# A hybrid decoder step on one core: prompt attention's steps taken two by two, w_in's blocks in another order, the cached sums moved into a triangular product, and the first sequence's rows fetched during prompt attention

## The chip, the cores and the metric

The kernel runs on one core of one Trainium2 chip. The metric is the device time of one execution in microseconds (us), median of the runs shown. The profile comes from one further execution of the same program.

## What is computed

One inference step of a one-layer decoder for a prompt of 512 tokens and for 8 sample sequences of 8 new tokens each, whose 2048 cached tokens lie in pages of 128. Both groups share the weights (D_MODEL 1024, 8 heads of 64, two key/value groups for each attention). The reference, cut to what matters here:

```python
mod = silu(c) @ w_ada + b_ada                       # six parts: shift, scale, gate, twice
h = rms_norm(x) * (1 + sc1) + sh1
z = h @ w_in                                        # fox q,k,v,f; nsa q, kv (6 parts), gates; two merge gates
logf = log_sigmoid(ff + b_fox_f)
fox:  softmax(q k / 8 + cumsum(logf)_q - cumsum(logf)_k) v         # causal
nsa:  gate0 * compressed + gate1 * selected + gate2 * window       # each a softmax with alibi bias
mix = g_fox * (o_fox @ w_br_fox) + g_nsa * (o_nsa @ w_br_nsa)
x = x + gt1 * (mix @ w_out)
y = x + gt2 * (relu(h2 @ w_up) ** 2 @ w_down)
```

The prompt has only 8 selection blocks for 16 places, so its selected attention is a causal one over all tokens. For the samples the compressed scores rank the cached blocks, 16 are selected, and fox needs, for each cached token, the sum of the log forget values of all later cached tokens (a suffix sum over 2048 tokens for each head). New key and value rows are outputs too.

## The kernel before, in words

Work goes through stages. Most products are made in pairs of high and low parts (`split`, line 130).

**First stage** (`first_stage`). 32 steps u = 0..31 (keys and values in turn): page rows (tile `cpg`) are put in order (`ro`), turned (`ct`), split (`xh`, `xl`) and multiplied (`hid`) to compress the cached keys and values. A table `todo` hangs other work on the steps, behind the step's own: the norm of x, and the first 8 of w_ada's 24 blocks, 1 MB each (`wada`, two buffers). `ada_first_load` issues a block's load on SP's queue, `ada_first` multiplies it (`ada`), `ada_end` turns and adds its parts (`adat`), and `modulate` then applies two blocks to the normed x. The modulated x (`hf`, 2.3 MB) is stored for a later stage (`hfd`).

**Projection** (`run`, `project`). Eight blocks of w_in's columns in the order of `WIN` (`z` matmuls). Each block's weights are asked for one block ahead (`win_load`, tile `winr`). Between blocks lie norms of heads (`head_norm`: squares on ScalarE, the rest on VectorE), stores of new rows (SP), the prompt's compressed keys (`cmp_prompt_a` to `_e`), one more w_ada block for each step (`ada_later`), and the copying of cached fox rows, a piece for each step, into an order fit for loading (`stage`, DRAM tensors `foxD`, `lfD`).

**Prompt attention** (`prompt_attention`). Twelve steps of one branch and one pair of heads each, in the order slc 0, win 0, slc 1, win 1, ..., win 3, then fox 0 to 3. A step makes the scores of both groups (`scores`: matmuls into PSUM, VectorE adds the bias row and takes the row minimum, ScalarE the exponential); in the next step its weights are turned (`turn_over`: TensorE into PSUM, ScalarE or VectorE copies `PT` out) and multiplied with the values (`weigh`, tile `oT`). A slc step has the compressed heads besides (`cmp_heads` on VectorE, from an accumulator bank `cs`; of those there are two, tag `acc`, and `weigh` uses one or two). `kstack` and `qstack` make stacked high and low keys and queries. Into this stage are put: for the prompt, fk's norm and the log-sigmoid (step 0), `decay` and `forget_rows` (fox's bias rows, over DRAM); for the samples, `sample_kv`, `forget_load` and `forget_sums` (suffix sums of the cached log forget values in `Dt`, by four doubling passes over 1024 columns on VectorE and one product over partitions), `sample_cmp`, `sample_rank`, `sample_select`. `ada_later` goes on until block 23; its room (`adw`, tag `r2`) is free then.

**Sample attention** (`sample_tables`, `sample_attention`). Tables first (one-hot `E`, `bhot`, masks `nbA`, `nbW`, the bias `ramp`). Then for each sequence two halves of 8 pages: `sample_load` (fox rows `fr` of 1 MB by one DMA, nsa rows `sr` by eight DMAs of 128 KB, all on SP), `sample_scores` one sequence ahead, and `sample_values`. A score block gets its decay by four matmuls of `E` with the turned `Dt` (`DT`). `hf` is read back (tile `hf1b`) ahead of the first rows. Then come the merge (`mix_part`), w_out and the MLP.

What sets the order: the program is written in the order above, and the scheduler of the tile framework orders each engine's instructions by a timeline that it simulates. `issue_after` and `behind` bind an instruction behind another on the same engine. `dma` keeps SP's transfers in the order of the program, and an instruction that waits holds all that are behind it on its engine or queue.

Of the kernel before, what the change touches and what calls it, by code (L numbers as in the profile page):

```python
# [14 lines left out]
P = 128  # L15
# [29 lines left out]
class Step:  # L45
# [268 lines left out]
    def ada_later(self):  # L314

        a = self.adw
        if self.ada_next:
            self.ada_next()
        ch = self.adn
        self.ada_next = None  # L320
# [4 lines left out]
        w = a[:, 2048 * e:2048 * e + 2048].rearrange("p (k c) -> p k c", k=NK)  # L325
        self.ada_load(ch, w)

        def later():
            part = a[:, 4096 + 256 * e:4352 + 256 * e]
            self.ada_sum(ch, w, part)  # L330
            self.ada_end(ch, part, a[:, 4608 + 18 * e:4626 + 18 * e].rearrange("p (j r) -> p j r", j=2))
# [159 lines left out]
    def first_stage(self, pl, pe, hf):  # L491
# [116 lines left out]
    def forget_sums(self, pa):  # L608
# [4 lines left out]
        fl = lambda t, a, e: t[:, :, a:e, :].rearrange("p b c h -> p b (c h)")  # L613
# [4 lines left out]
        cur, nxt = sc  # L618
        tot = self.carve([P, NB, 8])
        self.cp(tot, cur[:, :, 0, :])  # L620
        xb = self.accb("xsuf")
        self.mm(xb[:, 0:64], triS, tot.rearrange("p b h -> p (b h)"), True, True)
        self.cp(tot, xb[:, 0:64].rearrange("p (b h) -> p b h", h=8))
        self.tt(nxt[:, :, 0:15, :], cur[:, :, 1:16, :], tot[:, :, None, :].to_broadcast([P, NB, 15, 8]), OP.add)
        self.cp(nxt[:, :, 15, :], tot)
        self.cp(self.Dt, nxt)
# [118 lines left out]
    WIN = ((1288, 264), (1552, 264), (1816, 264), (0, 256), (256, 256), (776, 256), (1032, 256), (512, 264))  # L745
# [52 lines left out]
    def log_sigmoid(self, pz):  # L798
# [5 lines left out]
        e, u, l1, d = [pz.tile([P, 40], F32, name=f"ls{i}") for i in range(4)]  # L804
# [120 lines left out]
    def prompt_attention(self, pk, pn, pp):  # L925
# [16 lines left out]
        kst = {"slc": self.kslc, "win": self.kstack(pp, "win", C_WK)}  # L942
        qs = {("nsa", 0): self.qnsa}
        fox = {}
        prev = pcT = None
        for br, r in [(br, r) for r in range(4) for br in ("slc", "win")] + [("fox", r) for r in range(4)]:
# [4 lines left out]
            elif br == "fox":  # L951
                rows = fox[r]
# [22 lines left out]
            if (br, r) == ("win", 0):  # L975
                qs["nsa", 1] = self.qstack(pp, "nsa", C_NQ, 1, 1)
# [907 lines left out]
```

## Time and profile before

| | us |
|---|---|
| runs before | 1404.58, 1409.5, 1407.9; median 1407.9 |
| profiled execution | 1405.54 |
| its span | 1403.8 |
| first stage | 0 to about 200 |
| projection | about 200 to 334 |
| prompt attention | about 335 to 530 |
| sample attention | about 530 to 755 |
| merge, w_out, MLP | about 755 to 1404 |

How to read it: a row of the timeline has its start, its length, engine, line, operation, output tile, input tiles, shapes and count; in brackets at its end stands how long the engine had stood idle, and behind which engine's instruction or transfer. A row of the windows has the busy time of each engine in a stretch with the number of instructions, the granted clock of TensorE (1.00 is full), the share of the DMA engines and GB/s. PE is TensorE, PEld its weight load, DVE VectorE, ACT ScalarE, POOL GpSimd, SPq the issues of SyncE's queue. L76 is the helper for matmuls and L82 that for turns, so tiles tell more than lines.

### The profile page before, as it was taken

The numbers are of one execution on the slowest core, as the hardware profiler recorded it, in microseconds if no ns is written. First come the engines' busy times: TensorE is split into PE (matmuls) and PEld (weight loads), VectorE is DVE, ScalarE is ACT, GpSimd is POOL, SyncE is SP. The second block draws the span as 40 slices with busy tenths as digits, with TensorE's granted clock in tenths as the row PEclk, the third lists the DMA queues.
The fourth block names the chain that finished last, engine by engine and source line by source line (L and its number), as shares of the span: only waits on it lengthen the run. The fifth ranks groups of instructions, "written<-read, shape, count | busy, mean of one in ns | idle before, by whom it ended". The sixth has DMA issues, their size and how long they took to land.

```text
span 1403.8 us, 23571 instructions
## 1 busy us (share of the span) xinstructions
PE 1296.2 (92%) x8787; PEld 1060.3 (76%) x8787; DVE 729.5 (52%) x1910; ACT 504.5 (36%) x1097; POOL 89.9 (6%) x89
## 2 busy tenths in 40 slices
PE   1897999997898977999999999998899999999998
PEld 0776789896555543555558999998888998998997
DVE  3576675458756684344336433377523443443464
ACT  2344353245655642223226222232432321321320
POOL 0000000002211210000000000000100100100110
PEclk9999999998998988999999999999999999999999
DMA  9576256752235537565553533140422321331401
GB/s 206 164 220 191 78 177 224 249 194 93 82 106 148 154 134 249 201 210 192 198 165 102 133 83 91 53 121 1 150 63 74 116 77 49 120 89 33 120 31 68
DMA packets 167832, 182.78 MB, mean 130 GB/s; under 512 B 15813, under 2 KB 153326, under 8 KB 163366
## 3 DMA queue, kind: packets, MB, share of 16 engines
q1 hardware_dynamic: 162406, 178.14, 41.3%
q10 hardware_dynamic: 5312, 3.15, 1.0%
q8 instruction: 69, 1.13, 0.3%
q14 instruction: 45, 0.37, 0.1%
HBM read 169.99 MB, written 28.54 MB: 141 GB/s over the span
## 4 chain that ended last, share of the span: by engine, by line
PE 77%; SPq 6%; DMA 6%; DVE 6%; ACT 2%; issue 2%; POOL 0%; DVEq 0%; ACTq 0%
PE dn L76 14%; PE up L76 14%; PE mg L76 7%; PE z L76 7%; SPq L154 6%; PE ss L76 5%; PE hid L76 4%; PE br L76 4%; PE so L76 4%; PE wo L76 3%; PE ada L76 2%; PE ct L82 1%; DMA cpg<-in_cache_nsa_kv 1%; DMA sr<-in_cache_nsa_kv 1%; PE sp L82 1%
## 5 line engine op out<-in xcount | busy, mean ns | idle before, releaser
L76 PE MATMUL dn<-wdh,u 128*128 128x512 f32 x576 | 181.9, 390 | 0.0
L76 PEld LDWEIGHTS dn<-wdh,u 128*128 128x128 f32 x576 | 107.6, 188 | 21.9
L76 PE MATMUL dn<-wdl,u 128*128 128x512 f32 x320 | 123.6, 389 | 0.0
L76 PE MATMUL z<-winh,h 128*128 128x264 f32 (+1 forms) x576 | 113.1, 289 | 1.9 <-DVE h L708 1.7
L76 PE MATMUL up<-h,wuh 128*128 128x256 f32 x512 | 96.7, 282 | 4.3 <-ACT h L111 4.3
L76 PEld LDWEIGHTS z<-winh,h 128*128 128x128 f32 x576 | 93.2, 192 | 4.6 <-DVE h L708 2.9
L76 PE MATMUL z<-winl,h 128*128 128x264 f32 (+1 forms) x320 | 88.9, 286 | 0.0
L111 ACT ACTIVATE wdh<-wdr 128x1024 fp32r<-128x1024 f32 x32 | 33.1, 1054 | 148.6 <-PE dn L76 127.7
L76 PE MATMUL up<-h3H,wuh 128*128 128x320 f32 x256 | 80.6, 315 | 6.2 <-ACT wuh L111 6.2
L130 DVE TENSOR_TENSOR wul<-wur,wuh 128x1024 fp32r<-128x1024 f32 x32 | 48.9, 1534 | 70.9 <-ACT wuh L111 70.9
L99 DVE TENSOR_TENSOR acc<-acc,dn 128x512 f32<-128x512 f32 x60 | 40.3, 686 | 86.5 <-PE dn L76 86.5
L76 PEld LDWEIGHTS up<-h,wuh 128*128 128x128 f32 x512 | 81.4, 191 | 4.5 <-ACT h L111 4.5
L76 PE MATMUL up<-h3H,wul 128*128 128x320 f32 x256 | 80.1, 313 | 0.3 <-DVE wul L130 0.3
L76 PE MATMUL up<-h3L,wuh 128*128 128x320 f32 x256 | 79.9, 312 | 0.0
L76 PE MATMUL mg<-hH,wmh 128*128 128x288 f32 x256 | 75.4, 295 | 0.8 <-ACT hH L111 0.8
L76 PE MATMUL mg<-hL,wmh 128*128 128x288 f32 x256 | 74.6, 296 | 0.6 <-DVE hL L130 0.6
L76 PE MATMUL mg<-hH,wml 128*128 128x288 f32 x256 | 75.2, 294 | 0.0
L76 PE MATMUL up<-h,wul 128*128 128x256 f32 x256 | 72.1, 282 | 0.0
L1674 POOL TENSOR_TENSOR u<-u 128x576 f32<-128x576 f32 x32 | 43.5, 1361 | 439.5 <-ACT u L111 434.3
L82 PE MATMUL ct<-identF,ro 128*128 128x128 f32 x256 | 38.3, 297 | 35.4 <-DVE ro L114 29.8
L111 ACT ACTIVATE xh<-ct 128x256 fp32r<-128x256 f32 x128 | 47.7, 385 | 63.8 <-PE ct L82 41.7
L76 PEld LDWEIGHTS dn<-wdl,u 128*128 128x128 f32 x320 | 60.1, 188 | 12.6
(663 smaller groups left out, 3126.0 us busy)
## 6 DMA issues: line engine op xcount, KB each, us to landing
adw<-in_w_ada SPq DMA_DIRECT2D x16, 1024.0 KB
foxD<-in_cache_fox_kv SPq DMA_DIRECT2D x128, 128.0 KB
fr<-foxD SPq DMA_DIRECT2D x16, 1024.0 KB
sr<-in_cache_nsa_kv SPq DMA_DIRECT2D x128, 128.0 KB
wur<-in_w_up SPq DMA_DIRECT2D x32, 512.0 KB
wdr<-in_w_down SPq DMA_DIRECT2D x32, 512.0 KB
cpg<-in_cache_nsa_kv SPq DMA_DIRECT2D x120, 128.0 KB
wada<-in_w_ada SPq DMA_DIRECT2D x8, 1024.0 KB
```

The lines of the kernel that those rows point to most:

```text
L76: ins = self.nc.tensor.matmul(out, a, b, start=start, stop=stop, skip_group_check=True)
L82: ins = self.nc.tensor.transpose(out, in_, self.identF[:n, :n])
L99: self.nc.vector.tensor_tensor(out, a, b, op=op)
L111: return self.nc.scalar.activation(out, in_, f, **kw)
L130: self.splits.append((eng or self.nc.vector).tensor_tensor(l, x, h.bitcast(F32), op=OP.subtract).ins)
L154: self.issued[eng] = getattr(self.nc, eng).dma_start(out, in_).ins
L1674: nc.gpsimd.tensor_tensor(u[j], u[j], u[j], op=OP.mult)
```

## The change

Six things:

1. First stage: w_ada's third to eighth block are multiplied at u = 17, 19, 21, 23, 25, 27 instead of 14, 16, 18, 20, 21, 22, and loaded at u = 12, 14, 18, 20, 22, 24 instead of 10, 12, 15, 17, 19, 21. At 12 and 14 the load is written behind the 16 pages of sequences 6 and 7.
2. Projection: `WIN` in another order (fk, fv, ff and nsa's queries earlier, win's keys and fox's queries last), so fk's norm, the log-sigmoid and their stores, and group 0's and 1's stacked nsa queries (now wholly on VectorE) are made there; fox's queries are normed in two halves, the second in prompt attention, and `sample_q` for fox goes there.
3. Prompt attention: slc 0, slc 1, win 0, win 1, slc 2, slc 3, win 2, win 3, fox 0 to 3. Fox's stacked keys are made at step n = 5 instead of 6, its bias rows two steps ahead, `sample_select` within step 11. `ada_later` turns and adds a block one step later than it multiplies it.
4. `forget_sums`: VectorE adds only halves of 8 columns; `E` is no one-hot table now but has a one for each later column of the half, so that its matmuls (same number and shape) add them up.
5. Tables: `nbA` and `nbW` get their diagonal by 3 copies instead of 24; `ramp` is scaled on ScalarE by a factor that is zero for its lower rows, instead of a product and a memset on VectorE.
6. Sample attention: the first half of sequence 0 is loaded at step n = 9 into the room of w_ada's blocks; `hf` is read back into that room behind that half's values.

The core of the diff:

```diff
@@ first_stage
-        for k, u in enumerate((9, 11, 14, 16, 18, 20, 21, 22)):
+        for k, u in enumerate((9, 11, 17, 19, 21, 23, 25, 27)):
             todo[u] += [lambda k=k: ends.update({k: self.ada_first(pe, ada[k])})]
             todo[u + 1] += [lambda k=k: ends[k]()]
-            if k < 6:
-                todo[u + 1] += [lambda k=k: self.ada_first_load(pe, ada[k + 2])]
+            if k > 1:
+                todo[(12, 14, 18, 20, 22, 24)[k - 2]] += [lambda k=k: self.ada_first_load(pe, ada[k])]
@@ forget_sums
-        sc = [self.Dt, pa.tile([P, NB, 16, 8], F32, tag="wide", name="lf")]
...
-        for i, sh in enumerate((1, 2, 4, 8)):
-            cur, nxt = sc[i % 2], sc[(i + 1) % 2]
-            self.tt(fl(nxt, 0, 16 - sh), fl(cur, 0, 16 - sh), fl(cur, sh, 16), OP.add)
-            self.cp(fl(nxt, 16 - sh, 16), fl(cur, 16 - sh, 16))
...
+        with self.tc.issue_after(self.last_min):
+            self.nc.vector.tensor_reduce(half, self.Dt.rearrange("p b (a c) h -> p (b a) h c", a=2), axis=AX.X, op=OP.add)
...
+        self.cp(self.Dt[:, :, 8, :], xv)
+        self.tt(self.Dt[:, :, 0, :], xv, hv[:, :, 1], OP.add)
@@ project
-    WIN = ((1288, 264), (1552, 264), (1816, 264), (0, 256), (256, 256), (776, 256), (1032, 256), (512, 264))
+    WIN = ((1288, 264), (1552, 264), (512, 264), (776, 256), (1032, 256), (1816, 264), (0, 256), (256, 256))
@@ prompt_attention
-        for br, r in [(br, r) for r in range(4) for br in ("slc", "win")] + [("fox", r) for r in range(4)]:
+        steps = [(br, r) for a in (0, 2) for br in ("slc", "win") for r in (a, a + 1)] + [("fox", r) for r in range(4)]
+        for n, (br, r) in enumerate(steps):
...
+            if n == 0:
+                self.head_norm("fq1", C_FQ + 256, 4)
+                kst["win"] = self.kstack(pp, "win", C_WK)
+            if n == 1:
+                self.sample_q(self.bdF, C_FQ, 0)
+                self.sample_kv()
...
+            if n == 5:
+                kst["fox"] = self.kstack(pk, "fox", C_FK, "w1")
...
-            if (br, r) == ("slc", 0):
-                self.head_norm("fk", C_FK, 2, 0)
-                self.store_rows("fox", C_FK, 256)
-                self.log_sigmoid(pn)
...
+            if n == 11:
+                self.sample_select()
...
+            if 6 <= n < 10:
+                rows["fox", n - 6] = self.forget_rows(pp, n - 6)
...
+            if n == 9:
+                self.sample_rank()
...
+                self.sample_load(None, 0, 0)
+            if n == 10:
+                self.forget_sums()
@@ sample_tables
-        self.ts(self.E.rearrange("p c (h t) -> p (c h) t", t=8), ei[:, :, None].to_broadcast([P, 64, 8]), self.p63, None,
-                OP.is_equal)
...
+        self.ts(tok, ei[:, 0:8], lim, None, OP.is_lt)
+        self.ts(hot, ei[:, 0:8, None].to_broadcast([P, 8, 8]), self.t_row, None, OP.is_equal)
+        self.tt(self.E, tok[:, :, None].to_broadcast([P, 8, 64]),
+                hot.rearrange("p h t -> p (h t)")[:, None, :].to_broadcast([P, 8, 64]), OP.mult)
@@ sample_attention
-        for b in range(2):
-            for hf in range(2):
-                self.sample_load(sp, b, hf)
+        for b, hf in ((0, 1), (1, 0), (1, 1)):
+            self.sample_load(sp, b, hf)
...
+                if b + hf == 0:
+                    self.hf2 = self.keep.tile([P, NK, NT], F32, tag="r2", bufs=1, name="hf1b")
+                    self.dma("sync", self.hf2, self.hfd)
@@ run, the projection
             step(2)
-            self.head_norm("sk", C_SK, 2, 1)
             self.cmp_prompt_b(0)
             self.cmp_prompt_load(pk, 1)
+            self.head_norm("fk", C_FK, 2, 0)
+            self.log_sigmoid()
+            self.store_rows("fox", C_FK, 256)
             step(3)
...
+            step(5, between=[lambda: None] * 3 + [lambda: self.qnsa.update(self.qstack(pk, "nsa", C_NQ, 1, 0, (0,), True))])
...
+            step(6, between=[lambda: self.qnsa.update(self.qstack(pk, "nsa", C_NQ, 1, 0, (1,), True)), lambda: None,
+                             lambda: self.sample_q(self.bdN, C_NQ, 1)])
```

More of the change, by code (lines that the diff above doesn't have):

```diff
@@ L1042, in kstack, with qstack @@
         return out
-    def qstack(self, pp, which, c0, gi, rp, early=False):
+    def qstack(self, pp, which, c0, gi, rp, gs=(0, 1), early=False):
         st = {}
-        for g in range(2):
+        for g in gs:
             tb = self.trb(f"q{which}{rp}{g}")
@@ L1342, in sample_tables @@
         self.tt(nbf, self.nbf, tmask[:NS], OP.add)
[L1343 to L1344 removed]
+        self.nbA = sq.tile([P, NB * 72], F32, name="nbA")
+        self.nbW = sq.tile([NS, NB * 72], F32, name="nbW")
         gp.memset(self.nbA, NEG)
         gp.memset(self.nbW, NEG)
[L1347 to L1350 removed]
+        own = lambda t: t.rearrange("p (b x) -> p b x", x=72)[:, :, 0:8]
+        self.cp(own(self.nbA)[0:64], nbf)
+        self.cp(own(self.nbA)[64:128], tramp[64:128])
+        self.cp(own(self.nbW), tramp[0:64])
         wv = s1.tile([NS, 4, P], F32, name="wv")
@@ L1811, in run @@
         with ExitStack() as c:
-            hf = keep.tile([P, NK, NT], F32, tag="r2", bufs=1, name="hf1b")
-            nc.sync.dma_start(hf, self.hfd)
             sq = self.pool("sq", c)
```

143 lines of the change are left out of this document (67 added, 76 removed).

## The prediction

> **What bounds the kernel now.** I read the page's busy shares and its chain first, then the windows by stage, then who kept TensorE waiting.
>
> ```profile
> PE 1296.2 (92%) x8787; PEld 1060.3 (76%) x8787; DVE 729.5 (52%) x1910; ACT 504.5 (36%) x1097; POOL 89.9 (6%) x89
> PE 77%; SPq 6%; DMA 6%; DVE 6%; ACT 2%; issue 2%; POOL 0%; DVEq 0%; ACTq 0%
> ```
>
> TensorE is the bound, and the diff takes no matmul of weight away from it. So there is only something to win where TensorE waits, or runs at a lower granted clock after a wait. The windows show where that is (columns: length, busy time of each engine with its count, granted clock, DMA share, GB/s):
>
> ```profile
> 134.00:141.00 7.00, 0.88 (x12) 0.42 (x16) 0.31 (x1) 0.00 (x0) 0.00 (x0) 0.65 0.94 301
> 141.00:146.00 5.00, 5.00 (x30) 4.09 (x23) 0.92 (x3) 1.40 (x4) 0.00 (x0) 0.50 0.41 114
> 245.00:290.00 45.00, 43.48 (x413) 40.77 (x413) 20.46 (x57) 14.20 (x27) 0.00 (x0) 1.00 0.76 244
> 335.00:368.00 33.00, 24.18 (x151) 16.12 (x151) 28.10 (x113) 23.32 (x62) 6.30 (x9) 0.79 0.30 87
> 384.00:410.00 26.00, 25.70 (x188) 15.94 (x184) 15.53 (x61) 16.63 (x48) 2.04 (x2) 1.00 0.28 86
> 444.00:461.00 17.00, 13.03 (x52) 8.54 (x51) 11.62 (x28) 4.93 (x13) 0.00 (x0) 0.60 0.60 172
> 505.00:530.00 25.00, 19.65 (x96) 11.19 (x93) 17.57 (x58) 7.39 (x17) 4.90 (x8) 0.80 0.21 87
> 530.00:556.00 26.00, 19.92 (x86) 8.80 (x87) 13.24 (x39) 3.41 (x9) 0.00 (x0) 0.80 0.82 273
> 560.00:760.00 200.00, 198.27 (x1442) 113.45 (x1443) 82.77 (x269) 67.31 (x159) 0.00 (x0) 1.00 0.55 183
> ```
>
> The projection (the row from 245) and the steady part of sample attention (from 560) leave TensorE no gap worth naming, and a slc step with its win step costs 26 us at full clock (from 384). Five places are bad. As a measure of each I take its length less busy time times granted clock, which is what would be left over if the same matmuls ran without a gap at full clock: 134 to 146 us: 12 - (0.88 x 0.65 + 5.00 x 0.50) = 8.9. 335 to 368: 33 - 24.18 x 0.79 = 13.9. 444 to 461: 17 - 13.03 x 0.60 = 9.2. 505 to 530: 25 - 19.65 x 0.80 = 9.3. 530 to 556: 26 - 19.92 x 0.80 = 10.1. Together 51 us, estimates worked out from these rows. The timeline rows below carry in brackets how long an engine had stood and what ended it. The change touches each of them; the sum goes place by place.
>
> **Place 1, the fifth w_ada block (term A).** SP issues its transfers in order:
>
> ```profile
> 97.80 0.53 SPq L154 DMA_DIRECT2D wada<-in_w_ada  x1
> 99.16 14.71 SPq L154 DMA_DIRECT2D cpg<-in_cache_nsa_kv  x16
> 121.42 12.69 SPq L154 DMA_DIRECT2D cpg<-in_cache_nsa_kv  x16
> 126.58 0.71 PE L76 MATMUL hid<-xh,w1hlv 128*128 128x512 f32 x2
> 130.45 0.71 PE L76 MATMUL hid<-xh,w1hlk 128*128 128x512 f32 x2
> 134.20 1.16 SPq L154 DMA_DIRECT2D wada<-in_w_ada  x2
> 140.12 1.93 PE L76 MATMUL ada<-wada,adw 128*32 128x256 f32 x16 [6.63 <-DMA wada<-in_w_ada]
> ```
>
> TensorE reaches this block at 133.5 (140.12 - 6.63) and stands until 140.1, because the load goes out only behind 32 cache pages. With the new table the third block is loaded where the fourth was and the fourth where the fifth was, and the fourth is multiplied at u=19, not the fifth at u=18. Its load goes out some 1.4 to 3.4 us earlier (one block fewer ahead: 99.16 - 97.80, and perhaps 14.71 - 12.69 of contention), so at 131 to 133, and lands 5.9 us later (140.1 - 134.2) at the latest: 137 to 139. TensorE gets there at about 136: 133.5, less one product that now comes later (1.07, below), plus one hidden step with its turns (130.45 - 126.58 = 3.9). Blocks five to eight go out three steps ahead each and are early. Left is a wait of 0 to 3 us. What a short wait does to the clock is seen earlier in this stage:
>
> ```profile
> 87.38 1.18 PE L82 MATMUL nt<-identF,x 128*128 128x128 f32 x8 [1.99 <-DVE x L103]
> 88.49 1.94 PE L76 MATMUL ada<-wada,adw 128*32 128x256 f32 x16
> 101.11 1.07 PE L76 MATMUL ada<-wada,adw 128*32 128x256 f32 x16
> ```
>
> After 1.99 us without work the same 16 matmuls took 1.94 us, not 1.07: the clock was already down, and so a rest of 2 us costs some 2 us of slow matmuls beside itself. I take A = 6.5, a rest of a good 1 us with some loss of clock, between 8.9 (no wait left) and 4 (3 us and a cold clock).
>
> [...]
>
> **Place 2, the start of prompt attention (term B).**
>
> ```profile
> 338.57 1.28 ACT L111 ACT_TABLE_LOAD   x1
> 340.12 1.28 ACT L111 ACT_TABLE_LOAD   x1
> 345.20 0.47 PE L76 MATMUL sslc<-khslc,qstnsa 128*128 128x128 f32 x1 [5.03 <-POOL qstnsa L1059]
> ```
>
> Group 1's stacked query is finished by GpSimd only at 345, since ScalarE loads two tables for the log-sigmoid ahead of it. In the change both groups' stacks are made by VectorE during blocks 5 and 6, and fk's norm, the log-sigmoid and its table loads lie beneath the projection, where ACT was busy 14.20 of 45 us. So this 5.0 us wait goes. What is late next is VectorE: 28.10 of 33 us busy here, and it keeps most of its load, as fq's second half is normed in place of fk, win's keys are still stacked, the zeroing for sample_q comes in, and slc 1, now the second step, brings the compressed heads that win 0 did not have. TensorE's wait ends, VectorE's queue does not. I take B = 4, with 0 (VectorE as long as before) and 10 (only 4 us of the 13.9 stay) as ends.
>
> **Place 3, fox's stacked keys (term C).**
>
> ```profile
> 445.34 1.16 DVE L99 TENSOR_TENSOR lf<-Dt 128x960 f32<-128x960 f32 x1 [2.35 <-DMA Dt<-lfD]
> 447.79 1.51 PE L76 MATMUL sfox<-khfox,qstfox 128*128 128x128 f32 x4 [3.64 <-DVE khfox L114]
> ```
>
> The planner put the first op of the cached sums ahead of khfox on VectorE; it waits for Dt's load, the keys behind it wait as well, and TensorE then runs at clock 0.60 until 461. The change makes the keys two steps earlier (n = 5) and binds the sums behind the last row minimum of step 10, so neither stands ahead of fox's first scores. I take C = 8 of 9.2; the low end is 5, should the clock still dip at some other wait there.
>
> **Place 4, the end of prompt attention (term D).**
>
> ```profile
> 507.29 1.16 PE L76 MATMUL selx<-scr 128*32 128x512 f32 x2 [2.07 <-DVE scr L105]
> 510.89 1.16 DVE L99 TENSOR_TENSOR lf<-Dt,scr 128x960 f32<-128x960 f32 x1
> 513.75 2.35 DVE L103 TENSOR_SCALAR bhot<-ei,prow 32x512 bf16<-32x512 f32 x4
> 516.92 0.55 PE L82 MATMUL ptfox<-identF,Sfox 128*128 128x128 f32 x3 [1.86 <-DVE PTfox L114]
> L114 DVE COPY nbA<-tramp 64x8 f32<-64x8 f32 x8 | 1.3, 169 | 0.1
> ```
>
> Three things stood ahead of fox 2's and fox 3's turned weights: the ranks (2.07 us), the rest of the sums (1.16 and two copies, some 2 us), and the tables. The selection now comes a step after the ranks, the sums shrink to one reduce of 1024 elements (1.1 us by the like-sized op above) and three small ops, as E's matmuls, unchanged in number, add up the suffix; and 24 copies of 8 columns (three groups of 1.3 us) become 3 copies of 64. About 6 us leave VectorE; bhot stays in its way. D = 5, ends 1 and 9.
>
> **Place 5, first sequence of sample attention (term E).**
>
> ```profile
> 503.03 0.44 SPq L1813 DMA_DIRECT2D hf1b<-hfd  x1
> 528.23 0.66 PE L82 MATMUL fcfox<-identF,ffox 128*128 128x128 f32 x4
> 529.61 0.32 SPq L154 DMA_DIRECT2D fr<-foxD  x1
> 534.87 1.09 PE L82 MATMUL fk<-identF,fr 128*128 128x128 f32 x4 [3.64 <-DMA fr<-foxD]
> 543.64 0.65 PE L82 MATMUL fk<-identF,fr 128*128 128x128 f32 x4
> 547.41 0.66 PE L82 MATMUL fk<-identF,fr 128*128 128x128 f32 x4
> 555.86 0.63 PE L82 MATMUL fk<-identF,fr 128*128 128x128 f32 x4 [0.94 <-DMA fr<-foxD]
> ```
>
> The first rows are asked for when the last fox matmul lets their room go (529.6), and the scores of sequence 1 begin at 555.9, 26.2 us later. With half 0 already in the finished w_ada room, the scores of sequence 0 start at once: four quarters of 3.77 us (547.41 - 543.64) and about 4 us for window, new tokens and DT make 19. E = 7. Half 1 is issued at about 529 and lands, like half 0 did, 6 to 8 us later, when its first quarter is due (after 8 us): just in time. Ends: 3 if it is late, 9 if a turn or two slips in before the end of fox 3. hf's second load leaves the place ahead of fox's last staging and goes behind the values of half 0; sample attention has DMA at 0.55, so it hides, and is needed only at 760. Uncovered it would cost its 2.3 MB at 273 GB/s, 8 us.
>
> **New waits (term F).** slc after slc asks for three accumulator banks of two: the values of slc 0 wait until VectorE has read slc 1's compressed scores (estimated at 0 to 2 us, twice, by the 2.07 us above for a like wait on VectorE). The stores of fk and logf stand on SP ahead of w_ada, staging and the next w_in block, and SP stands at them until the norm is done; the nearest row is the z stage with its own stores, 1.5 us of 45 idle. Reordered work of the prompt may open small gaps. F = -2, ends 0 and -8 (both banks, and three such idle stretches of 1.5 us).
>
> Sum: 6.5 + 4 + 8 + 5 + 7 - 2 = 28.5 us. The profiled execution took 1405.5 us (span 1403.8), so 1377; the median shown is 1407.9, 2.4 higher and within its spread of 5. I forecast **1377**. All upper ends together (8.9 + 10 + 9.2 + 9 + 9) give 46 and 1359; all lower ones (4 + 0 + 5 + 1 + 3 - 8) give 5 and 1400.
>
> **Rivals.** (1) VectorE takes over prompt attention: B and D come to nothing and F doubles. For it: 28.10 of 33 us busy at the start. Against it: 15.53 of 26 in the steady pair. Gain 28.5 - 9 - 2 = 17.5, 1388. (2) All five places close, with F as it is: 46 - 2 = 44, 1361; against it, that VectorE's queue has to follow. (3) Slower: SP starves the projection. A store that waits for its norm holds the w_in block behind it, and five blocks lie behind moved stores. The chain of waits already passes one block by this way:
>
> ```profile
> 257.55 9.25 DMA foxD<-in_cache_fox_kv
> 266.86 4.01 DMA winr<-in_w_in
> ```
>
> If each of five blocks came 8 us late, 40 us would go, and the time be 1416; it decides from 6 us a block. Against it: a block is issued one block ahead, and TensorE idled only 1.5 us of 45 there with stores on the queue. (4) The order on the engines is the planner's, and what it opens elsewhere eats what it closes: 1405, within 0.3%.
>
> **How the numbers follow.** Forecast (1368 to 1385) 0.60; rival 1 (1385 to 1396) 0.20; rival 2 0.07; rival 3 0.07; rival 4 0.06, half of it inside 0.3% (4 us, about what a measurement of this kernel can tell from no change), the rest shared. Faster 0.60 + 0.20 + 0.07 + 0.015 = 0.885, same 0.03, slower 0.07 + 0.015 = 0.085. The range of 8 in 10 takes in the forecast, rival 1 and the near part of rival 2: 1360 to 1394.
>
> **What would show it.** A: the fifth w_ada product without a 6.6 us wait, and no row of clock 0.5 between 134 and 146. B: no wait for qstnsa after the first scores; the first values of slc at about 25 to 29 us after the first scores instead of 33. C: fox's first scores at full clock, and no op of Dt ahead of khfox. D: no gap over 1 us for selx or PTfox. E: fk of sequence 1 about 19 us after the last fox matmul. The forecast is wrong if a new wait of several us with a cold clock stands in the projection or between the slc steps, or if half 1 lands late.

## The result, and the profile after

The changed kernel took 1370.09 us (median of 4 runs, 1367.88 to 1374.93) against 1408.7 us for the kernel before in the same series: a ratio of 0.9736, 95% interval 0.9703 to 0.9769. In a second series, beside experiments, the same program took 1366.45 us against 1410.04: 0.9691, 0.9667 to 0.9716. So the change gains 39 to 44 us, where 28.5 were forecast (1377, range 1360 to 1394).

The profiled execution of the changed kernel has a span of 1373.1 us; it is the slowest of the first series (1374.93 us). Its page, busy shares and chain:

```profile
PE 1288.1 (94%) x8787; PEld 1053.9 (77%) x8787; DVE 722.8 (53%) x1929; ACT 505.7 (37%) x1108; POOL 84.4 (6%) x85
PE 84%; DVE 7%; DMA 3%; SPq 2%; ACT 2%; issue 1%; DVEq 0%; ACTq 0%
```

TensorE's share of the chain rose from 77% to 84%; SP's queue went from 6% to 2%, transfers from 6% to 3%, and VectorE from 6% to 7%. Where the time went is read best by stage. The windows below run between the same events in each kernel: start, first `z`, first scores of slc 0, first values of slc 0, first fox scores, last turn of fox, first `mg` of the merge. Columns as in the prediction. The kernel before:

```profile
0.00:200.43 200.43, 153.64 (x955) 123.12 (x956) 118.14 (x391) 77.24 (x182) 0.53 (x6) 0.96 0.61 171
200.43:335.23 134.80, 130.93 (x1145) 123.51 (x1143) 78.42 (x235) 52.28 (x112) 1.43 (x1) 0.99 0.63 205
335.23:368.02 32.79, 24.20 (x151) 16.12 (x151) 27.87 (x112) 23.27 (x61) 6.13 (x8) 0.79 0.30 88
368.02:447.79 79.77, 71.68 (x518) 43.84 (x517) 51.01 (x184) 48.32 (x135) 15.27 (x16) 0.99 0.35 103
447.79:528.23 80.44, 70.09 (x404) 43.39 (x404) 58.52 (x186) 39.04 (x106) 12.98 (x19) 0.86 0.47 148
528.23:755.66 227.43, 217.94 (x1524) 120.78 (x1523) 93.41 (x308) 71.26 (x175) 0.00 (x0) 0.98 0.59 195
```

The changed kernel, profiled execution:

```profile
0.00:195.42 195.42, 154.06 (x955) 123.90 (x956) 118.88 (x391) 77.04 (x182) 1.70 (x8) 0.96 0.61 174
195.42:327.45 132.03, 129.61 (x1142) 121.73 (x1140) 86.12 (x297) 53.45 (x119) 1.45 (x3) 1.00 0.67 216
327.45:357.37 29.92, 26.14 (x165) 17.28 (x162) 24.66 (x105) 22.14 (x65) 0.00 (x0) 0.83 0.25 76
357.37:434.65 77.28, 72.75 (x518) 43.49 (x517) 49.76 (x174) 48.56 (x136) 15.20 (x16) 0.98 0.30 88
434.65:507.60 72.95, 63.52 (x400) 38.90 (x398) 50.72 (x160) 38.23 (x104) 12.49 (x19) 0.93 0.61 179
507.60:726.54 218.94, 214.27 (x1523) 119.25 (x1523) 90.50 (x307) 73.28 (x176) 0.00 (x0) 1.00 0.61 203
```

The same program once more, with a span of 1363.1 us (the run e11_after_again below; at 1364.82 us the fastest of the second series, so the two profiles stand for the two ends of what the program does):

```profile
0.00:190.22 190.22, 151.30 (x956) 121.60 (x956) 118.52 (x391) 77.06 (x182) 1.70 (x8) 0.97 0.63 179
190.22:322.23 132.01, 130.11 (x1141) 123.12 (x1140) 86.55 (x297) 53.89 (x119) 1.45 (x3) 0.99 0.67 216
322.23:349.63 27.40, 23.13 (x165) 15.62 (x162) 24.62 (x105) 21.64 (x65) 0.00 (x0) 0.94 0.27 83
349.63:425.13 75.50, 70.95 (x518) 43.05 (x517) 49.77 (x174) 48.97 (x137) 15.19 (x16) 1.00 0.29 90
425.13:495.50 70.37, 62.20 (x400) 38.71 (x398) 50.52 (x160) 38.46 (x104) 12.49 (x19) 0.95 0.62 184
495.50:714.43 218.93, 214.25 (x1524) 119.24 (x1523) 90.49 (x307) 73.28 (x176) 0.00 (x0) 1.00 0.61 204
```

Two things can be worked out from each row: TensorE's **rest** (length less its busy time) and the **lost clock** (busy time times one less the granted clock, good to a microsecond in the long stages, as the clock has two digits).

| stage | length: before, after, again | rest | lost clock |
|---|---|---|---|
| first stage | 200.4, 195.4, 190.2 | 46.8, 41.4, 38.9 | 6.1, 6.2, 4.5 |
| projection | 134.8, 132.0, 132.0 | 3.9, 2.4, 1.9 | 1.3, 0, 1.3 |
| start of prompt attention | 32.8, 29.9, 27.4 | 8.6, 3.8, 4.3 | 5.1, 4.4, 1.4 |
| slc and win steps | 79.8, 77.3, 75.5 | 8.1, 4.5, 4.5 | 0.7, 1.5, 0 |
| fox steps | 80.4, 73.0, 70.4 | 10.3, 9.4, 8.2 | 9.8, 4.4, 3.1 |
| sample attention | 227.4, 218.9, 218.9 | 9.5, 4.7, 4.7 | 4.4, 0, 0 |

After sample attention nothing changed: 1403.8 - 755.66 = 648.1 us before, 646.6 and 648.7 after. Every stage the forecast named became shorter, and the projection as well. The third column of lengths is the surprise: the same program is 12.1 us shorter up to the merge in one execution than in another, 5.2 of it in the first stage and 6.9 in prompt attention.

### The profile page after: what moved, and what is told of

It is laid out like the page before. It is cut to its first block, busy times and chain, and to the rows that moved or that the text cites. A ratio compares the mean times of both kernels' runs of the same rounds, so it can differ in the third digit from the quotient of the medians.

```text
span 1373.1 us, 23604 instructions
## 1 busy us (share of the span) xinstructions
PE 1288.1 (94%) x8787; PEld 1053.9 (77%) x8787; DVE 722.8 (53%) x1929; ACT 505.7 (37%) x1108; POOL 84.4 (6%) x85
## 4 chain that ended last, share of the span: by engine, by line
PE 84%; DVE 7%; DMA 3%; SPq 2%; ACT 2%; issue 1%; DVEq 0%; ACTq 0%
PE dn L76 15%; PE up L76 14%; PE z L76 8%; PE mg L76 7%; PE ss L76 6%; PE hid L76 5%; PE br L76 4%; PE so L76 4%; PE wo L76 3%; PE ada L76 2%; PE ct L82 2%; SPq L154 2%; PE fk L82 1%; DMA cpg<-in_cache_nsa_kv 1%; PE sp L82 1%
## 5 line engine op out<-in xcount | busy, mean ns | idle before, releaser
L76 PE MATMUL z<-winl,h 128*128 128x256 f32 (+1 forms) x320 | 88.2, 284 | 0.0
```

Of the source, the lines that this page charges most:

```text
L76: ins = self.nc.tensor.matmul(out, a, b, start=start, stop=stop, skip_group_check=True)
```

## The experiments

My theory is the forecast's: five separate places where TensorE rests and then runs at half clock, each opened by its own edit. The rival is that a few edits do all of it, or that VectorE sets the pace and the edits only move its work. Seven kernels undo one part of the change, one does a single part in the kernel before, three try to improve on it, one repeats it. Each ratio is to the kernel before in the same series; the changed kernel's is 0.9691 (0.9667 to 0.9716) in the series of e9 to e12. A thousandth is 1.4 us, and with intervals of 0.0025 to each side two kernels differ surely from about 0.004 on. From one series to another even that says little, for the changed kernel's own two ratios, 0.9736 and 0.9691, are 0.0045 apart. So stage lengths are read beside the ratios.

**e1_old_table**: the first stage's table undone.

```diff
-        for k, u in enumerate((9, 11, 17, 19, 21, 23, 25, 27)):
+        for k, u in enumerate((9, 11, 14, 16, 18, 20, 21, 22)):
...
-            if k > 1:
-                todo[(12, 14, 18, 20, 22, 24)[k - 2]] += [lambda k=k: self.ada_first_load(pe, ada[k])]
+            if k < 6:
+                todo[u + 1] += [lambda k=k: self.ada_first_load(pe, ada[k + 2])]
```

> The changed kernel with the old table of w_ada blocks in the first stage. My theory (term A, and the milestones of the two profiles): the fifth block again waits 6.6 us behind 32 cache pages and the first stage ends at 200.4 instead of 195.4 in the span, so 5 us later; nothing after it makes that up, so the time is about 1375 (5 us above the changed kernel's 1370). Rival, that a later w_in block or w_ada block would have held the projection anyway: first stage at 200.4, but the end of the projection within 1 us of the changed kernel's 326.2, time about 1370.

Measured 1376.76 us, ratio 0.9749 (0.9724 to 0.9774). First stage 200.1 us, projection 132.0 as in the changed kernel: the loss is passed on whole, and the rival falls. The wait is back, in a timeline row of this run:

```profile
138.75 1.94 PE L76 MATMUL ada<-wada,adw 128*32 128x256 f32 x16 [6.81 <-DMA wada<-in_w_ada]
```

Against the changed kernel's two ratios that is 0.0013 and 0.0058 more, 2 to 8 us. The stage itself says it better: the three profiles with the old table (the kernel before, this run, e8) have a first stage of 200.1 to 202.0 us, the nine with the change's table and order of loads 189.5 to 195.4.

**e2_logsig_late**: fk's norm, the log-sigmoid and their stores go from the projection to step 0 of prompt attention.

```diff
-            self.head_norm("fk", C_FK, 2, 0)
-            self.log_sigmoid()
-            self.store_rows("fox", C_FK, 256)
             step(3)
...
             if n == 0:
+                self.head_norm("fk", C_FK, 2, 0)
+                self.log_sigmoid()
+                self.store_rows("fox", C_FK, 256)
```

> The changed kernel with fk's norm, the log-sigmoid and fk's stores put back into the first step of prompt attention; the stacked queries stay in the projection. Theory (VectorE is the bound of the start, busy 9.8 of 10 us between 335 and 345): some 33 operations or 6 us of VectorE come on top, and two table loads on ScalarE; the values of slc 0 begin 35 to 38 us after the first scores instead of 30.0, and the time goes to 1374 to 1378. Rival (only the 5.0 us wait for the query stacked by GpSimd mattered, as my term B had it): those operations hide, the values begin 30 to 32 us after the first scores, time 1370 to 1372.

Measured 1367.15 us, 0.9685 (0.9660 to 0.9710), and the values of slc 0 begin 30.0 us after the first scores, against 29.9 and 27.4: no loss that shows. But this does not speak for the rival, for the work did not go where the edit wrote it. Two rows of VectorE's timeline in this run, and its window from first scores to first values:

```profile
239.85 0.16 DVE L99 TENSOR_TENSOR logf<-r1w,bfox 64x8 f32<-64x8 f32 x1
317.26 0.88 DVE L99 TENSOR_TENSOR zF<-zF,kgain 128x128 f32<-128x128 f32 x4
321.50:351.48 29.98, 26.20 (x165) 17.25 (x161) 24.65 (x105) 22.04 (x65) 0.00 (x0) 0.83 0.25 76
```

The log-sigmoid is under way at 239.9 and fk's norm ends at 318, both beneath the projection, and VectorE does the same 105 operations in the start as in the changed kernel. With fk and ff in w_in's third block, the planner finds room for them there even when the program names them in prompt attention. So it is the order of the blocks that allowed this, and the place in the text did not matter. What it would cost in the start is not shown.

**e10_qstack_old**: slc's first stacked queries are made again in the last block's step, their second halves on GpSimd.

```diff
-            step(5, between=[lambda: None] * 3 + [lambda: self.qnsa.update(self.qstack(pk, "nsa", C_NQ, 1, 0, (0,), True))])
+            step(5)
...
-            step(7)
+            def turned():
+                self.qnsa = self.qstack(pk, "nsa", C_NQ, 1, 0, (0, 1), True)
+
+            step(7, between=[lambda: None] * 2 + [turned])
...
-                eng.tensor_tensor(s[hi], tmp[lo], s[lo].bitcast(F32), op=OP.subtract)
+                self.nc.gpsimd.tensor_tensor(s[hi], tmp[lo], s[lo].bitcast(F32), op=OP.subtract)
```

> The changed kernel with the stacked queries of slc 0 made in the last block's step and their second halves on GpSimd, as before; the new order of w_in's blocks stays. Theory (the wait of 5.0 us for that stack was the cause of term B, and half of it is the late place): the first scores of group 1 wait for GpSimd 2 to 5 us, and the values of slc 0 begin 31 to 33 us after the first scores instead of 27.4 to 30. Rival (the new order of blocks has the queries ready so early that the place does not matter): no wait for the stack, 27 to 30 us.

Measured 1374.26 us, 0.9739 (0.9717 to 0.9761). The start takes 34.8 us instead of 29.9 or 27.4, so the place of the queries (with the engine that stacks them) is worth 5 to 7 us, but not by the wait that I named: GpSimd is done in time, and TensorE waits for no stack. Window of the start, a row of the timeline, and the window at half clock around it:

```profile
322.82:357.59 34.77, 29.46 (x166) 19.12 (x162) 25.86 (x107) 21.82 (x64) 3.01 (x4) 0.71 0.21 66
345.07 1.06 PE L82 MATMUL ct<-identF,cP 128*64 128x128 f32 x4 [2.87 <-DVE cP L99]
343.73:357.39 13.66, 12.17 (x47) 7.79 (x47) 5.66 (x25) 7.37 (x21) 0.00 (x0) 0.50 0.02 4
```

VectorE now does the compressed heads (`cP`) 3.4 us later after the first scores than in the repeat, TensorE rests 2.87 us for them, and runs at clock 0.50 from 343.7 to 357.4; another 6.8 us at half clock (333.5 to 340.3) lie ahead of that rest. The stage's rest is 5.3 us, 1.0 more than in the repeat; its lost clock is 8.5 instead of 1.4. So nearly all of the 7 us against the repeat is clock. By which path the place of the queries makes `cP` late is not shown.

**e8_before_bound**: one thing alone, in the kernel before: the doubling passes bound behind step 10's last row minimum.

```diff
-            self.tt(fl(nxt, 0, 16 - sh), fl(cur, 0, 16 - sh), fl(cur, sh, 16), OP.add)
-            self.cp(fl(nxt, 16 - sh, 16), fl(cur, 16 - sh, 16))
+            with self.tc.issue_after(self.last_min):
+                self.tt(fl(nxt, 0, 16 - sh), fl(cur, 0, 16 - sh), fl(cur, sh, 16), OP.add)
+                self.cp(fl(nxt, 16 - sh, 16), fl(cur, 16 - sh, 16))
```

> The kernel before with one thing of the change: the doubling passes of the cached sums are bound behind the last row minimum of step 10, so they stand behind fox's keys on VectorE. Theory (term C: the passes that waited for Dt's load ahead of the keys were the cause): no wait for the keys, first fox scores 3 to 4 us earlier against the first scores of slc 0 (112.6 us in the kernel before), the first fox step at full clock; 5 to 8 us faster than before. Rival (the keys are late of themselves, being made only at the step before): the wait stays over 2 us and the time is within 2 us of before.

Measured 1405.39 us against 1410.51, ratio 0.9956 (0.9936 to 0.9977): some 5 to 6 us faster, as the theory had it. The first fox scores come 108.9 us after the first scores instead of 112.6. The first 13 us of fox in the kernel before, and the same with the bond, whose row of the first scores follows:

```profile
447.79:460.79 13.00, 12.67 (x48) 8.38 (x48) 9.22 (x24) 4.37 (x13) 0.00 (x0) 0.52 0.55 176
```

```profile
446.01:459.01 13.00, 12.72 (x88) 7.71 (x88) 8.25 (x28) 8.04 (x24) 0.00 (x0) 1.00 0.69 197
446.01 0.88 PE L76 MATMUL sfox<-khfox,qstfox 128*128 128x128 f32 x4 [0.57 <-DVE khfox L114]
```

TensorE is as busy in both, but does 88 matmul records instead of 48. Yet the fox steps as a whole go only from 80.4 to 79.6 us: the passes now stand ahead of the samples' compressed scores (`cpt`), for which TensorE waits 4.0 us. The bond moves the sums; it takes the change's fourth edit to make them small.

**e3_sums_free**: the bond taken away in the changed kernel (the line `with self.tc.issue_after(self.last_min):` around the reduce).

> The changed kernel without the bond of the sums' first operation to the last row minimum of step 10. Theory of term C as I wrote it (the bond keeps the sums away from the keys): without it the reduce stands early on VectorE's queue and waits for Dt's load, TensorE waits 3 to 4 us with a cold clock, +4 to +6 us, 1375. Rival (the keys made two steps earlier do it alone): the reduce comes at most a step earlier, after Dt has landed, the first fox scores wait for nothing, and the time is within 2 us of 1370; it may even be better, since the reduce then leaves the compressed scores of the samples.

Measured 1369.35 us, 0.9694 (0.9671 to 0.9718); first fox scores 107.2 us after the first scores, fox steps 73.2 us. The rival holds: with the keys made at step 5, fox's first scores wait for nothing without the bond. The reduce now runs at 458.2, ahead of a row minimum of the next step, for which TensorE waits 1.9 us, and in exchange the wait for the samples' compressed scores falls from 2.1 to 1.0 us. So term C has two ways of being had, the bond (e8) or the earlier keys (e3); in the changed kernel the bond only chooses which wait stays.

**e9_sums_doubling**: the four passes and the one-hot table again, bound as the reduce was (the removed lines of the diff's `forget_sums` and `sample_tables` put back).

> The changed kernel with the four doubling passes and the one-hot table again, bound behind the same row minimum as the changed kernel's reduce. Theory (term D, a part of it): 7.2 us of VectorE by the rows of the kernel before stand where 2.6 stood, in a stretch where VectorE is busy 9.9 of 10 us, and TensorE waits about 4 us for the samples' compressed scores instead of 2.1: from the first fox scores to the last fox turn 75 to 78 us instead of 71 to 73. Rival (the passes hide, since the samples' ranks have slack): 71 to 73.5 us.

Measured 1374.48 us, 0.9744 (0.9720 to 0.9768); fox steps 76.8 us against 73.0 and 70.4 in the changed kernel's two profiles. Its longest wait there:

```profile
PE cpt L82 <- DVE scr L114: 4.1, 1, 4.1
```

The theory holds: 4.6 us less of VectorE's work ahead of the ranks is worth 4 to 6 us of fox steps, and 8 us of the time in the same series (1374.48 against 1366.45).

**e7_sums_behind_ranks**: the reduce bound behind the last operation of the ranks.

```diff
-        with self.tc.issue_after(self.last_min):
+        with self.tc.issue_after(self.last_rank):
```

> The changed kernel with the sums' reduce bound behind the last operation of the ranks instead of the last row minimum of step 10. Theory (that 2.0 us reduce stands ahead of the samples' compressed scores, for which TensorE waits 2.1 us, with a clock of 0.66 behind it): the wait for the compressed scores falls below 0.5 us, and from the first fox scores to the last fox turn it takes 69 to 71 us instead of 73. Rival (VectorE is full there anyway, and the reduce only moves its 2 us to the turned weights of fox 3): another wait of 1.5 to 2.5 us takes its place, 72 to 74 us.

Measured 1372.01 us, 0.9740 (0.9714 to 0.9766); fox steps 76.2 us, 3 to 6 us longer than the changed kernel's. The wait for the compressed scores falls from 2.1 to 1.1 us, and two others take its place:

```profile
PE ptfox L82 <- DVE PTfox L114: 2.6, 2, 2.4
PE xsuf L76 <- DVE scr L99: 2.4, 1, 2.4
```

The rival holds, and more than it: so late, the reduce stands straight ahead of its own product (`xsuf`), for which TensorE waits 2.4 us.

**e4_no_prefetch**: sequence 0's first half loaded at the start of sample attention, and x read back ahead of it.

```diff
-                self.sample_load(None, 0, 0)
...
-        for b, hf in ((0, 1), (1, 0), (1, 1)):
+        for b, hf in ((0, 0), (0, 1), (1, 0), (1, 1)):
```

> The changed kernel with the first half of sequence 0 loaded at the start of sample attention, and the stored x read back ahead of it, as before. Theory (term E): TensorE waits 3.6 us for the first rows again, and from the last fox values' turn to the scores of sequence 1 it takes 26 to 28 us instead of 20.8: about 1377, 6 to 7 us above the changed kernel. Rival (the rows are then loaded beneath a shorter end of prompt attention, and it is VectorE's tables that hold the first scores): 20 to 22 us and 1370 to 1372.

Measured 1377.23 us, 0.9758 (0.9731 to 0.9784). From the last fox turn to the scores of sequence 1 it takes 524.46 - 498.87 = 25.6 us, and to the merge 227.2 us against 218.9 with the prefetch. Rows of this run:

```profile
498.87 0.66 PE L82 MATMUL fcfox<-identF,ffox 128*128 128x128 f32 x4
503.72 0.63 PE L82 MATMUL fk<-identF,fr 128*128 128x128 f32 x4 [1.73 <-DMA fr<-foxD]
508.04 1.12 PE L82 MATMUL fk<-identF,fr 128*128 128x128 f32 x4
524.46 0.63 PE L82 MATMUL fk<-identF,fr 128*128 128x128 f32 x4 [0.93 <-DMA fr<-foxD]
498.87:726.04 227.17, 219.31 (x1524) 120.75 (x1523) 90.94 (x307) 72.96 (x176) 0.00 (x0) 0.98 0.59 195
```

The theory holds, though the wait for the first rows is 1.7 us here and not 3.6. The price is 8 us of the stage rather than 6 to 7: TensorE waits for rows a second time at sequence 1, and the clock falls in between (1.12 us for the same four turns that took 0.63).

**e5_alternate**: the steps in the old alternating order.

```diff
-        steps = [(br, r) for a in (0, 2) for br in ("slc", "win") for r in (a, a + 1)] + [("fox", r) for r in range(4)]
+        steps = [(br, r) for r in range(4) for br in ("slc", "win")] + [("fox", r) for r in range(4)]
```

> The changed kernel with the steps in the old alternating order slc 0, win 0, slc 1, win 1 and so on; all else stays. Theory (VectorE is the bound of the start, and pairing gives nothing): slc 1's compressed heads, some 5 us of VectorE, leave the first 20 us, so the values of slc 0 begin 26 to 29 us after the first scores instead of 30, and prompt attention is as long as the changed kernel's 180 us from first scores to the last fox turn, or 1 to 4 us shorter. Rival (the pairing itself is worth a part of B): the values begin later than 31 us, prompt attention is 184 us or longer.

Its window of the start:

```profile
323.51:350.27 26.76, 24.14 (x157) 15.61 (x154) 22.31 (x93) 21.51 (x64) 0.00 (x0) 0.87 0.28 85
```

Measured 1370.4 us, 0.9728 (0.9702 to 0.9754). The start takes 26.8 us and prompt attention 176.3, between the changed kernel's 180.2 and 173.3 in its two executions. Its rest there is 16.1 us (2.6 + 4.7 + 8.8) against 17.7 and 17.0. The ratio is 0.0037 above the changed kernel's, which the intervals do not separate. What the pairing is worth stays open; by the ratios it is between nothing and 5 us, so the edit that the title names first is not what makes the kernel fast.

**e6_wada_early**: the fourth w_ada block asked for ahead of sequence 7's pages.

```diff
+        todo[14] += [lambda: self.ada_first_load(pe, ada[3])]
         for b, u in ((4, 4), (5, 6), (6, 12), (7, 14)):
...
-            if k > 1:
+            if k > 1 and k != 3:
```

> The changed kernel with the fourth w_ada block asked for ahead of the 16 pages of sequence 7 instead of behind them. Theory (the 2.6 us rest at the fourth block, with the 3.2 us of matmuls at half clock behind it, is all that is left of place 1): the load lands some 12 us earlier, the rest goes, and the first stage ends 3 to 4.5 us earlier counted from the step before that block; no row of clock 0.5 between 134 and 150. Rival (the stage is bound by the transfers themselves): the pages of sequence 7 come 2 to 3 us later and TensorE waits for them instead, 0 to 1 us gained.

Measured 1365.9 us, 0.9691 (0.9666 to 0.9716): the changed kernel's own ratio in its second series. The block's load is issued at 117.9 instead of 132.4 and its wait is gone, but the first stage, 190.9 us, is 4.5 us shorter only against the profile shown (195.4) and no shorter than the 190.2 of the repeat. Neither side of my expectation was right, for the wait that it removes is not always there (term A in the next section).

**e11_after_again**: the changed kernel repeated.

> The changed kernel once more, as a measure of what the same program does from one execution to the next and of the others of this call. If the clock after a rest of 1 to 3 us is a matter of chance, as equal orders of instructions with unequal clocks in the runs so far suggest, the first stage ends anywhere from 191 to 195.5 us in the span and prompt attention takes 175.5 to 180.5 us from first scores to last fox turn; if it follows from the program, both repeat within 1 us the profile shown (195.4 and 180.2).

Measured 1366.45 us, 0.9691; first stage 190.2, prompt attention 173.3: outside of even the lower end that I gave by 1 to 2 us. It is a difference between executions, not between programs.

**e12_combo**: e6's and e2's edits, and the halves added by three operations on GpSimd.

```diff
-        half = self.carve([P, 2 * NB, 8])
-        with self.tc.issue_after(self.last_min):
-            self.nc.vector.tensor_reduce(half, self.Dt.rearrange("p b (a c) h -> p (b a) h c", a=2), axis=AX.X, op=OP.add)
+        part = pa.tile([P, 2 * NB, 64], F32, tag="wide", name="part")
+        add = lambda o, t, n: self.nc.gpsimd.tensor_tensor(o, t[:, :, 0:n], t[:, :, n:2 * n], op=OP.add)
+        add(part[:, :, 0:32], self.Dt.rearrange("p b (a c) h -> p (b a) (c h)", a=2), 32)
+        add(part[:, :, 0:16], part, 16)
+        half = part[:, :, 0:8]
+        add(half, part, 8)
```

> The changed kernel with three edits: the fourth w_ada block asked for ahead of sequence 7's pages; fk's norm and the log-sigmoid in the first step of prompt attention; the halves of the sums added by three operations on GpSimd instead of one reduce on VectorE. Theory: the first takes 0 to 4.5 us, the second 1.7 us out of the projection at no cost behind it, the third the 2.1 us wait for the samples' compressed scores with what clock it costs: from first fox scores to last fox turn 69 to 71 us, and about 1363 to 1367 us. Rival (GpSimd's additions hold VectorE up, or the queries of fox 2 behind them come late): a new wait in fox's steps, 73 us or more there, 1368 or more.

Measured 1365.15 us, 0.9674 (0.9649 to 0.9700). The fox steps take 69.1 us against 70.4. The wait for the compressed scores, which I expected to go, is 1.1 us instead of 2.1, and the rival's wait for queries stacked on GpSimd is there, with 0.5 us (at 444.4). The 1.7 us that I expected in the projection came from a misread start of it in e2, whose first product ran at 189.5: the stage is 132.1 us here and 132.0 there. It beats the kernel before, and cannot be told from the changed kernel.

## Why the prediction was right, and where it was off

The sign, the places and the mechanism were right, and the time lies in the range; the sum of 28.5 us was 10 us or more too small against the medians (39 and 44). Against the two profiles, which are 30.7 and 40.7 us shorter than the one before, it was 2 and 12 too small; that it comes so near to the first is partly luck, since A to D were forecast 5.6 us too large for that execution and E and F 6.3 too small. By its terms:

- **A, the fifth w_ada block, 6.5.** The first stage gained 5.0 us in the profile shown and 10.2 in the repeat (e1's stage agrees). The forecast of "a wait of 0 to 3 us" with perhaps a cold clock was met: the fourth block is the late one. That no row of clock 0.5 would be left did not come true in the first profile. The price of a short rest was read too high: the two products of its row differ by 0.9 us (1.94 - 1.07), not by some 2. SP's row and the product there, then the product in e4, then in e5 (all three with the same program in the first stage):

```profile
132.40 0.54 SPq L154 DMA_DIRECT2D wada<-in_w_ada  x1
139.52 1.94 PE L76 MATMUL ada<-wada,adw 128*32 128x256 f32 x16 [2.60 <-DMA wada<-in_w_ada]
```

```profile
138.41 1.07 PE L76 MATMUL ada<-wada,adw 128*32 128x256 f32 x16 [2.54 <-DMA wada<-in_w_ada]
```

```profile
138.48 1.07 PE L76 MATMUL ada<-wada,adw 128*32 128x256 f32 x16
```

  The first two have nearly the same rest, 2.6 and 2.5 us, and one goes cold; in the third TensorE finds the block landed. In the nine profiles with this table and order of loads the rest here is nothing in four and 1.2 to 2.6 us in five, and the product is cold in two of those. That is why e6, which removes the rest, gains nothing that shows.
- **B, the start, 4.** Measured 2.9 and 5.4 us (32.8 to 29.9 and 27.4). The 5.0 us wait for GpSimd went, and the place of the queries is worth 5 to 7 us (e10); the log-sigmoid's share was not separated (e2). Rival 1 named the right engine for this stage, but not the right price: the rests that remain here are VectorE's (`nmslc`, `cP`), VectorE is busy 24.6 of 27.4 us, and with 2.3 us less of its work (e5) TensorE rests 2.6 us instead of 4.3; yet B did not come to nothing, and neither did D.
- **C, fox's keys, 8, and D, the ranks and tables, 5.** Together 13 forecast; the slc, win and fox stages gained 10.0 and 14.3. C alone is 5 to 6 us in the kernel before (e8), smaller than my 8, as the sums then stand ahead of the compressed scores; the small sums alone are worth 4 to 6 in the fox steps (e9), about what I gave to all of D. Of D's signs, the 2.07 us wait for the ranks is gone, and the one for turned weights fell from 1.86 to 1.14 us, not below 1; the wait for the samples' compressed scores rose from 0.8 to 2.1. That comes from their reduce, which was mis-sized: I took 1.1 us for 1024 elements, from an addition of like size. It took 2.0 us, and stands ahead of the ranks:

```profile
469.81 2.02 DVE L617 TENSOR_REDUCE scr<-Dt 128x128 f32<-128x1024 f32 x1
475.12 0.68 PE L82 MATMUL cpt<-identF,scr 128*127 128x128 f32 x4 [2.06 <-DVE scr L99]
```

- **E, the first rows, 7.** Measured 6.8 to the scores of sequence 1 (27.6 to 20.8 from the last fox turn) and 8.5 to the merge: I had stopped counting at sequence 1. Half 1, issued at 507.43, was in time; in the kernel before, half 0 was multiplied 5.3 us after its issue (534.87 - 529.61), sooner than the 6 to 8 us that I had assumed:

```profile
507.43 0.34 SPq L154 DMA_DIRECT2D fr<-foxD  x1
507.60 0.65 PE L82 MATMUL fcfox<-identF,ffox 128*128 128x128 f32 x4
510.44 0.62 PE L82 MATMUL fk<-identF,rows 128*128 128x128 f32 x4
528.41 0.66 PE L82 MATMUL fk<-identF,fr 128*128 128x128 f32 x4
```

- **F, new waits, -2.** This step failed, in its sign: the waits that it feared did not open. The stores on SP held up no w_in block (rival 3, whose time should have read 1417, 40 above 1377), the third accumulator bank shows in no wait, and the projection became 2.8 us shorter. Of that, 1.5 us are a wait that I had not looked up in the kernel before: `ada_later` turned a block in the step of its product, and TensorE stood for ScalarE's copy. The change turns it a step later, and the row has no partner after:

```profile
PE adat L82 <- ACT adw L111: 1.5, 1, 1.5
```

What separates the two executions is more clock than rest. By the table TensorE's rests sum to 87.2 us before and 66.2 and 62.5 after; the clock loses 27.4 us before, 16.5 in one execution of the changed kernel and 10.3 in the other. In A I had let a remaining rest pay for a cold stretch too, and that is what the repeat does not pay.

## What to carry to other kernels

Look for rests of 1.5 us and more in a kernel bound by TensorE (half clock stood behind one of 1.58 us here), and for shorter ones within 3.4 us of each other (behind some of at most 0.69 us as well), and remove the whole rest: what it cost beside itself in these runs hung on where it fell in the clock's time grid (next section), from nothing behind 2.5 us in e4 to 6.8 us at half clock behind 2.6 us in the profile shown. Before an experiment is read, look in its trace whether the work went where the edit wrote it: a planner may have moved it back. Where a stage repeats to 3 us from one execution to the next, compare stages of several executions before a microsecond is put down to an edit.

## What the runs showed of the hardware

In these runs the clock after a rest does not follow from the rest's length. The start of prompt attention has the same order of instructions in the changed kernel's two executions. The profile shown, with two windows around the row, then the repeat:

```profile
338.80 0.33 PE L76 MATMUL sslc<-khslc,qstnsa 128*128 128x128 f32 x1 [1.58 <-DVE nmslc L1091]
337.06:340.47 3.41, 1.60 (x11) 1.13 (x10) 3.35 (x14) 1.84 (x8) 0.00 (x0) 1.00 0.04 7
340.47:343.89 3.42, 3.42 (x22) 1.42 (x21) 3.36 (x19) 2.68 (x10) 0.00 (x0) 0.50 0.58 186
```

```profile
333.59 0.43 PE L76 MATMUL sslc<-khslc,qstnsa 128*128 128x128 f32 x1 [1.58 <-DVE nmslc L1091]
```

After the same 1.58 us the repeat goes cold at once (0.43 us for a product of 0.33, half clock from 333.66 to 337.07); the profile shown is still warm, goes cold from 340.47 to 343.89, and a second time from 350.71 to 357.54.

What I had taken for chance is the place of the rest on a grid of time. Up to 760 us, every stretch of clock 0.50 in the fourteen profiles lasts 3.41 us or two, three or four times that, and within one profile all begin on one grid of 3.41 us. The fourth w_ada block shows what that does: pieces of this grid around it in the profile shown, then in e4.

```profile
135.67:139.09 3.42, 1.25 (x6) 0.69 (x4) 1.66 (x10) 0.00 (x0) 0.00 (x0) 1.00 0.50 160
139.09:145.91 6.82, 6.39 (x35) 4.92 (x36) 2.68 (x6) 0.77 (x2) 0.00 (x0) 0.50 0.51 161
```

```profile
133.61:137.03 3.42, 2.26 (x10) 1.51 (x8) 2.66 (x16) 0.77 (x2) 0.00 (x0) 1.00 0.89 287
137.03:140.44 3.41, 2.03 (x25) 1.45 (x26) 0.76 (x2) 0.00 (x0) 0.00 (x0) 1.00 0.08 18
```

In the first, 2.2 us of the rest of 2.6 fall into one piece, TensorE is busy only 1.25 us of it, and the next two are at half clock. In e4 the rest of 2.5 us is shared by two pieces, the clock is 1.00 in both, and the product takes 1.07 us. Over all fourteen profiles, from 100 to 760 us, each of the 33 pieces at full clock with less than 1.6 us of busy TensorE was followed by one at half clock (busy time by the profile's records); of the 169 with 1.6 to 2.6 us busy 45 were, and of the 2379 with more none (in the profiles of the kernel before and of the changed one alone: 7 of 7, 7 of 23, none of 325). So in this program short rests within one piece count together: the piece ahead of 350.71 in the profile shown has 2.49 us of busy TensorE and no single rest over 0.69 us. Between 1.6 and 2.6 us busy time alone does not decide. One piece at half clock loses up to 1.7 us (half of 3.41, an estimate), and the start had one, two or three of them in the ten profiles with its steps and queries: 27.4 us long with one or two, 29.8 to 30.0 with three.

An addition of 512 elements took GpSimd 1.27 us in e12, and the two smaller ones behind it 1.06 and 0.45; the product that needs their sum (`xsuf`, at 475.44) stands there without a wait. The reduce of 1024 elements took VectorE 2.02 us, nearly twice an addition over 960 (1.16). It is not the reducing that is dear: in the same profile a reduce of 900 elements that lie side by side took 1.04 us. The elements that the sums' reduce adds lie 8 apart; that this view is the cause is a guess of mine that was not shown, as no run changes it alone.

```profile
486.78 1.04 DVE L1272 TENSOR_REDUCE scr<-scr 128x30 f32<-128x900 f32 x1
```
